# Front of a hybrid attention layer: value weights loaded and projected ahead of the queries and keys

## The chip, the cores and the metric

The kernel runs on one core of one Trainium2 chip. The metric is the device time of one execution in microseconds. Engines: PE is the tensor engine (matmuls and transposes), with its weight loads as PEld; DVE is the vector engine, ACT the scalar engine, POOL is GpSimd, and SP issues most DMAs. Each works through its own instructions in a fixed order; semaphores order the engines against each other.

## The reference

One layer over 1024 tokens of width 1024, all in float32:

```python
xn = rmsnorm(x, norm1_g[layer])
u = xn @ w_in[layer].astype(f32)
...
q_sb, k_sb, v_sb, f_raw, i_hg, q_hg, g_hg, gate_sb, gate_hg = jnp.split(u, list(c), axis=-1)
o_sb = stick_breaking_attention(split_heads(q_sb, SB_HEADS), split_heads(k_sb, SB_HEADS),
                                split_heads(v_sb, SB_HEADS))
...
merged = g_a * (o_sb @ w_o_sb[layer].astype(f32)) + g_b * (o_hg @ w_o_hg[layer].astype(f32))
h = x.astype(f32) + merged @ w_out[layer].astype(f32)
hn = rmsnorm(h, norm2_g[layer])
a = jnp.square(jax.nn.relu(hn @ w_ff1[layer].astype(f32)))
h = h + a @ w_ff2[layer].astype(f32)
```

A final `rmsnorm` follows. The change concerns the first two lines alone: the norm of the tokens, and the projections to the values of all 8 attention heads (512 columns of `w_in`) and to query and key of head 0 (64 columns each).

## The kernel before, in words

Tokens lie in 8 row blocks of 128 (`xt[0]` to `xt[7]`, tiles `x0` to `x7`), the width of 1024 in 8 k-blocks (`kt`). For full precision every operand of a projection is split into a high part in PE's format and a remainder: `hi_copy` casts on ACT (line 156), `lo_sub` subtracts on DVE (line 161), and a projection has three matmuls per k-block: high by high, remainder by high, high by remainder.

The front, for row blocks 0 to 3, goes like this. `first_norms` takes blocks 0 and 1: each block's sum of squares is made half on ACT (`n1scr`, line 629), half on DVE (line 281), added on DVE (`n_ms`, line 1284), raised to -1/2 on POOL (`n_y`, line 274), and multiplied into the block. `norm_transpose` has PE transpose the blocks into PSUM (`xnt`, one bank of PSUM for each k-block, line 131); ACT evicts the high part with the gain (`xnh`, line 348), DVE the remainder (`xnl`, line 351), both for two row blocks at once (256 columns). `u_qk0` is head 0's query and key weights (`wqk0r` as loaded, `wqk0whi` and `wqk0wlo` split), four DMAs of 128 KB; `u_v` the value weights, four tiles of 1024 columns (`wvr`, `wvh`, `wvl`, numbers 0 to 3), each with two k-blocks.

`first_job` writes PE's order of the projections as a generator; `st.advance(n, 1)` lets it go n steps on between the other stages. Before, it projects queries and keys (`pjqk`) of row blocks 0 and 1; then the values (`pjv`) of blocks 0 and 1 for the first four k-blocks, all matmuls with the high weights first, then those with the remainders; then queries and keys of blocks 2 and 3; then the other value k-blocks, and values of blocks 2 and 3. Row blocks 4 to 7 follow in the same way, half as many stages.

ACT and DVE stand in a fixed order in the front: `in_turn` chains each engine's instructions in the order in which they are written. `load` does the same for the DMAs of SP. An instruction that waits therefore holds up all that is written behind it on its engine. The order of the loads and of the stages is written out at the end of the kernel:

```python
    u_qk0.load()
    u_v.load(1)
    load_x(2)
    u_v.load(2)
    load_x(3)
    u_v.load()
...
    norm_transpose(xn, 0, 0, 2, lambda: keep_warm(1))
    st.advance(4, 1)
    u_v.split(2)
    norm1((2, 3), half_means((2, 3)))
```

Of the kernel before, what the change touches and what calls it, by code (L numbers as in the profile page):

```python
# [9 lines left out]
F32 = mybir.dt.float32  # L10
# [9 lines left out]
P = 128  # L20
# [19 lines left out]
def kernel(  # L40
# [230 lines left out]

    def inv_root(mean, name):
        y = small.tile([P, 1], F32, tag="rs_y1", name=f"{name}_y", bufs=4)
        nc.gpsimd.tensor_tensor(out=y, in0=mean, in1=expo[:, 0:1], op=ALU.pow)
        return y

    def mean_square(scr, src, before, name):
# [7 lines left out]
        )  # L285
        return out

    last_power = [None]

    last_evac = [None]  # L290

# [27 lines left out]
            c = (kt % 2) * 512 + (tb % 4) * P  # L319
            return h[:, c : c + P], l[:, c : c + P]  # L320

    def norm_transpose(acts, half, b0, n, between=None):

        banks = {}

        def turn_block(kt, b):
            if kt not in banks:
                banks[kt] = bank(f"xnt{half}{kt}_{b0}")[:, 0 : n * P]
            open_block("main")
            transpose(  # L330
                banks[kt][:, b * P : (b + 1) * P],
                xt[4 * half + b0 + b][:, kt * P : (kt + 1) * P],
            )

        ahead = 6 if between else 0
        for kt in range(ahead):
            turn_block(kt, 0)
        if between:
            between()
        for kt in range(KT):  # L340
            hi, lo = acts.t.get((half, kt // 2)) or acts.make(half, kt // 2)
            cs = slice(kt % 2 * 512 + b0 * P, kt % 2 * 512 + (b0 + n) * P)
            for b in range(n):
                if b > 0 or kt >= ahead:
                    turn_block(kt, b)
            pb = banks[kt]
            g = prm[:, G1 + kt : G1 + kt + 1]
            in_turn("act", nc.scalar.activation(hi[:, cs], pb, AF.Identity, scale=g))
            in_turn(
                "dve",  # L350
                nc.vector.scalar_tensor_tensor(
                    out=lo[:, cs],
                    in0=pb,
                    scalar=g,
                    in1=hi[:, cs].bitcast(F32),
                    op0=ALU.mult,
                    op1=ALU.subtract,
                ),
            )

    class Quads:

# [82 lines left out]
    class Unit:  # L445
# [192 lines left out]
    def first_norms(tbs):  # L638
        (l, lc), (r, rc) = halves()
        means = half_means(tbs)  # L640
        for tb in tbs:
            first = tb == tbs[0]
            if first:
                t = xt[tb][:, rc]
                in_turn("act", nc.scalar.activation(t, t, AF.Copy, scale=means[tb]))
# [12 lines left out]
    def norm1(tbs, means=None):  # L658
        for tb in tbs:
            t = xt[tb]  # L660
            r = means[tb] if means else token_rstd(t, f"n1_{tb}", slot(f"n1scr{tb}"))
            in_turn(
                "dve",
                nc.vector.tensor_scalar(out=t, in0=t, scalar1=r, scalar2=None, op0=ALU.mult),
            )
# [35 lines left out]
    class FirstUnit(Unit):  # L701
# [13 lines left out]
                ]  # L715

        def split(self, part=None):
            if part is None:
                return
            cs = slice(part * 512, (part + 1) * 512)  # L720
            (h, l), r = self.hl[0], self.raw[0]
            hi_lo(h[:, cs], l[:, cs], r[:, cs])

    def first_job():
        name, u_qk, ep = qk_item(0)
# [2 lines left out]
        u_v.roomy = range(4)  # L728
        open_banks = {}

        def v_part(tb, kt, hi=True, lo=True):
            if kt == 0 and hi:
                open_banks[tb] = bank(f"pjv_{tb}")
            ps = open_banks[tb]
            sh, sl = xn.stat(kt, tb)
            wh, wl = (w[:, kt % 2 * 512 : (kt % 2 + 1) * 512] for w in u_v.hl[kt // 2])
            if hi:
                matmul(ps, sh, wh, start=kt == 0, stop=False)
                matmul(ps, sl, wh, start=False, stop=False)
# [35 lines left out]
        return st.add([u_qk], body), u_qk, u_v  # L775

    j_first, u_qk0, u_v = first_job()
    j_qk = {0: j_first}

    QB_ORDER = (7, 0, 6, 1, 5, 2, 4, 3)  # L780
# [1546 lines left out]
    load_vectors(1, 6)  # L2327
    turns["on"] = True
    first_norms((0, 1))
    open_block("main")  # L2330
    keep_warm(1)
    norm_transpose(xn, 0, 0, 2, lambda: keep_warm(1))
    st.advance(4, 1)
    u_v.split(2)
    norm1((2, 3), half_means((2, 3)))
    lo_now()
    st.advance(3, 1)
    norm_transpose(xn, 0, 2, 2)
    u_v.split()
    st.advance(5, 1)  # L2340
    norm1(range(4, NT))
    st.advance(8, 1)
    norm_transpose(xn, 1, 0, 4)
# [169 lines left out]
```

## Time and profile before

| | us |
|---|---|
| three runs: median (lowest to highest) | 1420.89 (1420.53 to 1420.9) |
| the profiled execution: its own time | 1421.05 |
| the profiled execution: span | 1419.3 |
| PE busy | 1409.0 (99%) |
| DVE busy | 1087.3 (77%) |
| ACT busy | 684.4 (48%) |
| POOL busy | 147.9 (10%) |

Times in the profile's rows are microseconds from the start of the span. A row of the order of time has start, length, engine, source line, operation, output and inputs by the program's names without buffer numbers, shapes, and how many instructions it merges; a merged row's length reaches from the first start to the last end. In brackets stand the idle time of the engine just before, and what ended it. Matmuls overlap: one that lasts 0.39 us can be followed by the next after 0.23. So a busy PE is not PE at its peak, and paces are read from starts.

### The profile page before, as it was taken

The numbers are of one execution on the slowest core, as the hardware profiler recorded it, in microseconds if no ns is written. First come the engines' busy times: TensorE is split into PE (matmuls) and PEld (weight loads), VectorE is DVE, ScalarE is ACT, GpSimd is POOL, SyncE is SP. The second block draws the span as 40 slices with busy tenths as digits, with TensorE's granted clock in tenths as the row PEclk, the third lists the DMA queues.
The fourth block names the chain that finished last, engine by engine and source line by source line (L and its number), as shares of the span: only waits on it lengthen the run. The fifth ranks groups of instructions, "written<-read, shape, count | busy, mean of one in ns | idle before, by whom it ended". The sixth has DMA issues, their size and how long they took to land.

```text
span 1419.3 us, 18799 instructions
## 1 busy us (share of the span) xinstructions
PE 1409.0 (99%) x6848; PEld 1183.7 (83%) x6848; DVE 1087.3 (77%) x1494; ACT 684.4 (48%) x1181; POOL 147.9 (10%) x341
## 2 busy tenths in 40 slices
PE   9999999999999999999999999999999999999997
PEld 8888888888888888888888888888888888888886
DVE  7579988988567888887788897676666657768765
ACT  6356676664243554433344764445444443433343
POOL 3012223210011031000000300000000000000042
PEclk9999999999999999999999999999999999999999
DMA  7024445535135685364585514444446974776825
GB/s 243 26 67 127 106 99 98 107 77 155 60 74 174 221 223 182 123 213 156 163 297 193 185 58 166 163 163 145 140 141 242 355 259 154 275 278 239 275 98 179
DMA packets 163173, 237.72 MB, mean 167 GB/s; under 512 B 26332, under 2 KB 93448, under 8 KB 163080
## 3 DMA queue, kind: packets, MB, share of 16 engines
q1 hardware_dynamic: 146056, 190.37, 40.0%
q0 software_dynamic: 11584, 34.61, 10.0%
q10 hardware_dynamic: 5440, 11.54, 2.3%
q8 instruction: 54, 0.88, 0.2%
q14 instruction: 39, 0.32, 0.1%
HBM read 168.32 MB, written 66.06 MB: 165 GB/s over the span
## 4 chain that ended last, share of the span: by engine, by line
PE 98%; DVE 1%; ACT 1%; POOL 0%; DMA 0%; issue 0%; SPq 0%; DVEq 0%; ACTq 0%
PE pm L128 21%; PE pX L128 9%; PE pW L128 6%; PE pY L128 6%; PE pjqk L128 6%; PE pga L128 4%; PE gX L128 4%; PE gY L128 4%; PE pjf L128 3%; PE pjq L128 3%; PE pys L128 3%; PE pji L128 3%; PE pyh L128 3%; PE pjv L128 3%; PE po L128 3%; PE z L128 2%
## 5 line engine op out<-in xcount | busy, mean ns | idle before, releaser
L156 ACT CAST whid<-w 128x1024 fp32r<-128x1024 f32 x30 | 31.6, 1053 | 154.5 <-PE pm L128 89.8
L826 DVE TENSOR_TENSOR_SCAN rm<-rm,bits 128x511 f32<-128x511 f32 (+7 forms) x72 | 87.3, 1219 | 17.2 <-ACT rm L804 17.1
L128 PE MATMUL pm<-wlod,sh 128*128 128x512 f32 x240 | 93.5, 390 | 0.0
L128 PE MATMUL pm<-whid,sl 128*128 128x512 f32 x240 | 93.4, 389 | 0.0
L128 PE MATMUL pm<-whid,sh 128*128 128x512 f32 x240 | 93.4, 389 | 0.0
L128 PE MATMUL pm<-tl,sh 128*128 128x512 f32 (+1 forms) x210 | 81.3, 387 | 0.0
L128 PE MATMUL pm<-th,sl 128*128 128x512 f32 (+1 forms) x210 | 81.3, 387 | 0.0
L128 PE MATMUL pm<-th,sh 128*128 128x512 f32 (+1 forms) x210 | 81.3, 387 | 0.0
L161 DVE TENSOR_TENSOR wlod<-w,whid 128x1024 fp32r<-128x1024 f32 x30 | 36.7, 1222 | 55.2 <-ACT whid L156 55.1
L161 DVE TENSOR_TENSOR sl<-sa,sh 128x1024 fp32r<-128x1024 f32 x56 | 68.2, 1218 | 0.0
L156 ACT CAST wTh<-pw 128x512 fp32r<-128x512 f32 (+2 forms) x96 | 43.8, 485 | 41.9 <-PE pw L131 41.0
L2141 POOL TENSOR_SCALAR fss<-fss 128x1 f32<-128x1 f32 x8 | 4.5, 561 | 562.0 <-ACT fsc L2136 561.5
L156 ACT CAST sh<-sa 128x1024 fp32r<-128x1024 f32 x56 | 57.2, 1046 | 7.0 <-DMA sa<-ad 7.0
L128 PEld LDWEIGHTS pm<-wlod,sh 128*128 128x128 f32 x240 | 45.0, 187 | 9.9 <-DVE wlod L161 0.4
L128 PEld LDWEIGHTS pm<-whid,sh 128*128 128x128 f32 x240 | 45.1, 188 | 9.4
L161 DVE TENSOR_TENSOR wTl<-pw,wTh 128x512 fp32r<-128x512 f32 (+2 forms) x96 | 49.9, 546 | 3.9 <-ACT wTh L156 3.7
L128 PEld LDWEIGHTS pm<-whid,sl 128*128 128x128 f32 x240 | 45.1, 188 | 9.3
L169 DVE TENSOR_TENSOR bt<-bt,rm 128x511 f32<-128x511 f32 (+7 forms) x72 | 48.9, 684 | 3.5
L804 ACT ACTIVATE rm<-z 128x511 f32<-128x511 f32 (+4 forms) x96 | 48.0, 500 | 5.5 <-PE z L128 2.9
L128 PE MATMUL pX<-sql,t1h 128*128 128x512 f32 x128 | 49.9, 390 | 0.0
L128 PE MATMUL pX<-sqh,t1l 128*128 128x512 f32 x128 | 49.9, 390 | 0.0
L128 PE MATMUL pX<-sqh,t1h 128*128 128x512 f32 x128 | 49.8, 389 | 0.0
(930 smaller groups left out, 4435.9 us busy)
## 6 DMA issues: line engine op xcount, KB each, us to landing
w<-in_w_ff_dram SPq DMA_DIRECT2D x72, 512.0 KB, 4.8
sa<-ad SPq DMA_DIRECT2D x52, 512.0 KB, 6.4
ad<-a SPq DMA_DIRECT2D x32, 256.0 KB, 4.6
ad<-s SPq DMA_DIRECT2D x16, 512.0 KB, 3.3
tw<-in_w_out_dram POOLq DMA_DIRECT2D x24, 256.0 KB, 4.6
pr<-pd SPq DMA_DIRECT2D x10, 512.0 KB, 6.5
x<-in_x_dram SPq DMA_DIRECT2D x8, 512.0 KB, 7.8
xnl<-xnh POOLq DMA_DIRECT2D x8, 512.0 KB, 6.4
```

The costliest lines, as they stand in the source:

```text
L128: return pe(nc.tensor.matmul(*a, **k))
L156: hi_last[0] = after(in_turn("act", nc.scalar.copy(dst, src)), hi_behind[0])
L161: nc.vector.tensor_tensor(out=dst, in0=src, in1=hi.bitcast(F32), op=ALU.subtract),
L169: return nc.vector.tensor_tensor(out=out, in0=a, in1=b, op=ALU.mult)
L804: nc.scalar.activation(rm[:, s0 + c0 - 1 : s0 + m - 1], z[:, c0:m], AF.Sigmoid, scale=-0.125)
L826: sc = nc.vector.tensor_tensor_scan(out=rr, data0=rr, data1=bits[:, 1024 - nk + a : 1024 - nk + b][:, ::-1], initial=rm[:, b : b + 1] if i ...
L2141: nc.gpsimd.tensor_scalar(out=ssq, in0=ssq, scalar1=1.0 / D, scalar2=EPS, op0=ALU.mult, op1=ALU.add)
```

## The change

It reorders the front. (1) SP loads value weights 0 and 1 ahead of the query and key weights, and row blocks 2 and 3 behind those. (2) `first_norms` casts value weights 0 instead of the query and key weights; their remainders (`value_remainders`) are made half on DVE, half on POOL. (3) `norm_transpose` transposes all eight k-blocks of row block 0 before block 1, with two k-blocks in one PSUM bank (`paired`); value weights 1 are split between the fourth and the fifth k-block. (4) PE projects values of blocks 0 and 1 first, high weights, remainders of the tokens and remainders of the weights a quarter at a time (`v_quarter`), then queries and keys of blocks 0 and 1, then those of blocks 2 and 3 between the transposes of blocks 2 and 3. (5) The query and key weights are cast after the evictions; their remainders come on DVE after the mean of block 2. (6) The remainder of value weights 2 moves from DVE to POOL, and ACT takes half of block 3's norm.

```diff
@@ norm_transpose
+                pb = bank(f"xnt{half}{kt}_{b0}")
+                for i in range(1 + paired):
+                    banks[kt + i] = pb[:, i * n * P : (i + 1) * n * P]
...
-        ahead = 6 if between else 0
...
+            if then:
+                then(kt)
@@ Unit.split
-                if self.name == "wf1" or self.name == "wv" and i == 1:
+                if self.name == "wf1" or self.name == "wv" and i == 3:
                     hi_copy(h, r)
                     owed_wlo.append(lambda h=h, l=l, r=r: lo_sub(l, r, h))
                     continue
+                if self.name == "wv" and i == 2:
+                    hi_copy(h, r)
+                    ins = nc.gpsimd.tensor_tensor(
+                        out=l, in0=r, in1=h.bitcast(F32), op=ALU.subtract
+                    )
+                    after(ins, last_root[0])
+                    continue
@@ first_norms and what follows it
-        for part in range(2):
-            u_qk0.split(part)
+                split_values(0)
+
+    def split_values(i):
+        h, l = slot(f"wvh{i}", F32R), slot(f"wvl{i}", F32R)
+        u_v.hl = (u_v.hl or []) + [(h, l)]
+        raw = u_v.raw[i]
+        for _, cs in halves():
+            hi_copy(h[:, cs], raw[:, cs])
+
+    def value_remainders(i):
+        (h, l), raw = u_v.hl[i], u_v.raw[i]
+        (_, lc), (_, rc) = halves()
+        lo_sub(l[:, lc], raw[:, lc], h[:, lc])
+        nc.gpsimd.tensor_tensor(
+            out=l[:, rc], in0=raw[:, rc], in1=h[:, rc].bitcast(F32), op=ALU.subtract
+        )
@@ first_job
+        def v_quarter(k0):
+            for part in range(3):
+                for kt in (k0, k0 + 1):
+                    for tb in range(2):
+                        v_part(tb, kt, *(part == i for i in range(3)))
+                if part > 0:
+                    yield
...
         def body():
+            for k0 in (0, 2):
+                yield from v_quarter(k0)
             ps = bank(f"{name}_0")
             yield from qk_steps(ps, 0, 0, 2)
-            for hi in (True, False):
-                for k0 in (0, 2):
-                    for tb in range(2):
-                        for kt in (k0, k0 + 1):
-                            v_part(tb, kt, hi, not hi)
-                    yield
             yield from qk_steps(ps, 0, 2, 2)
@@ end of the kernel
+    u_v.load(2)
     u_qk0.load()
-    u_v.load(1)
     load_x(2)
-    u_v.load(2)
     load_x(3)
...
+    norm_transpose(xn, 0, 0, 2, lambda: keep_warm(1), second_values, 8, True)
+    for part in range(2):
+        u_qk0.split_hi(part)
+    means = half_means((2,))
+    for part in range(2):
+        u_qk0.split_lo(part)
+    means.update(half_means((3,)))
+    st.advance(8, 1)
+    u_v.split(3)
+    second_norms(means)
+    norm_transpose(
+        xn, 0, 2, 2, then=lambda kt: st.advance(1, 1) if kt in (4, 6, 7) else None, ahead=4
+    )
```

Where the instructions stand. First ACT, the evictions of row blocks 0 and 1, before; the two digits in `xnt00` are the half and the k-block, and the brackets name the engines whose semaphores an instruction waits for:

```order
L156 CAST wqk0whi_161<-wqk0r0_156 128x512 [waits DMAHW6_49,DMAHW5_49]
L348 ACTIVATE xnh00_229<-xnt00_0_216,prm_93 128x256 [waits PE_49]
L348 ACTIVATE xnh00_229<-xnt01_0_218,prm_93 128x256 [waits PE_49]
L348 ACTIVATE xnh01_237<-xnt02_0_220,prm_93 128x256 [waits PE_49]
L348 ACTIVATE xnh01_237<-xnt03_0_222,prm_93 128x256 [waits PE_49]
L348 ACTIVATE xnh02_245<-xnt04_0_224,prm_93 128x256 [waits PE_49]
```

The same place on ACT in the change:

```order
L156 CAST wvh0_210<-wvr0_156 128x512
L350 ACTIVATE xnh00_233<-xnt00_0_220,prm_93 128x256 [waits DVE_49,PE_49]
L350 ACTIVATE xnh00_233<-xnt00_0_220,prm_93 128x256 [waits DVE_49]
L350 ACTIVATE xnh01_241<-xnt02_0_223,prm_93 128x256 [waits PE_49]
L350 ACTIVATE xnh01_241<-xnt02_0_223,prm_93 128x256 [waits DVE_49]
L156 CAST wvh1_249<-wvr1_158 128x512 [waits DMAHW4_49]
L156 CAST wvh1_249<-wvr1_158 128x512
L350 ACTIVATE xnh02_255<-xnt04_0_226,prm_93 128x256 [waits PE_49]
```

Two evictions in a row now read one tile, and the second waits for DVE instead of PE; two casts stand among them.

On DVE, the mean of row block 2 in the change (`n1_2_ms` is DVE's half of it, `n1_2_ss` ACT's):

```order
L281 ISA n1scr2_273,n1_2_ms_276<-x2_167 128x512 [waits DMAHW1_49]
L281 ISA n1_2_ms_276 128x1
L1338 TENSOR_TENSOR n1_2_ms_276<-n1_2_ms_276,n1_2_ss_274 128x1 [waits DVE_49,Activation_49]
L161 TENSOR_TENSOR wqk0wlo_166<-wqk0r0_160,wqk0whi_165 128x512 [waits DMAHW6_49,DMAHW5_49]
L161 TENSOR_TENSOR wqk0wlo_166<-wqk0r0_160,wqk0whi_165 128x512 [waits DMAHW7_49,DMAHW0_49]
```

Before, the two `wqk0wlo` stood ahead of the first `xnl`, and values' remainders (`wvl0`) ahead of that mean; now `wqk0wlo` stands behind the sum that waits for ACT.

On PE, the first projection before:

```order
L131 MATMUL xnt07_0_260<-ident_75,x1_152 128x128
L128 MATMUL pjqk0_0_265<-xnh00_229,wqk0whi_161 128x256 [waits DVE_49]
L128 MATMUL pjqk0_0_265<-xnl00_230,wqk0whi_161 128x256
L128 MATMUL pjqk0_0_265<-xnh00_229,wqk0wlo_162 128x256
L128 MATMUL pjqk0_0_265<-xnh00_229,wqk0whi_161 128x256 [waits Activation_49]
```

and the end of the 24 value matmuls that stand in that place in the change, with the query and key matmuls behind them:

```order
L128 MATMUL pjv_0_217<-wvl1_250,xnh01_241 128x512 [waits Pool_49]
L128 MATMUL pjv_1_218<-wvl1_250,xnh01_241 128x512
L128 MATMUL pjqk0_0_315<-xnh00_233,wqk0whi_165 128x256 [waits Activation_49]
L128 MATMUL pjqk0_0_315<-xnl00_234,wqk0whi_165 128x256
L128 MATMUL pjqk0_0_315<-xnh00_233,wqk0wlo_166 128x256 [waits DVE_49]
L128 MATMUL pjqk0_0_315<-xnh00_233,wqk0whi_165 128x256
```

The first of these waits for ACT (the cast), the third for DVE (the remainder), each by itself.

More of the change, by code (lines that the diff above doesn't have):

```diff
@@ L273, in inv_root @@
         y = small.tile([P, 1], F32, tag="rs_y1", name=f"{name}_y", bufs=4)
-        nc.gpsimd.tensor_tensor(out=y, in0=mean, in1=expo[:, 0:1], op=ALU.pow)
+        last_root[0] = nc.gpsimd.tensor_tensor(out=y, in0=mean, in1=expo[:, 0:1], op=ALU.pow)
         return y
@@ L320, in stat, with norm_transpose @@
             return h[:, c : c + P], l[:, c : c + P]
-    def norm_transpose(acts, half, b0, n, between=None):
+    def norm_transpose(acts, half, b0, n, between=None, then=None, ahead=0, paired=False):
         banks = {}
@@ L327, in turn_block @@
             if kt not in banks:
-                banks[kt] = bank(f"xnt{half}{kt}_{b0}")[:, 0 : n * P]
+                pb = bank(f"xnt{half}{kt}_{b0}")
+                for i in range(1 + paired):
+                    banks[kt + i] = pb[:, i * n * P : (i + 1) * n * P]
             open_block("main")
@@ L342, in norm_transpose @@
             cs = slice(kt % 2 * 512 + b0 * P, kt % 2 * 512 + (b0 + n) * P)
-            for b in range(n):
-                if b > 0 or kt >= ahead:
-                    turn_block(kt, b)
+            for k in (kt, kt + 1)[: 1 + (kt + 1) % 2] if paired else (kt,):
+                for b in range(n):
+                    if (b > 0 or k >= ahead) and not (paired and kt % 2):
+                        turn_block(k, b)
             pb = banks[kt]
@@ L654, in first_norms, with second_norms, norm1 @@
                 turn_vectors(0, 1)
-        for part in range(2):
-            u_qk0.split(part)
-    def norm1(tbs, means=None):
+                split_values(0)
[12 more added lines that the diff above has]
+        )
+    def second_norms(means):
+        (l, lc), (r, rc) = halves()
+        for tb, cs in ((2, slice(None)), (3, lc)):
+            t = xt[tb][:, cs]
+            in_turn(
+                "dve",
+                nc.vector.tensor_scalar(
+                    out=t, in0=t, scalar1=means[tb], scalar2=None, op0=ALU.mult
+                ),
+            )
+        t = xt[3][:, rc]
+        in_turn("act", nc.scalar.activation(t, t, AF.Copy, scale=means[3]))
+    def norm1(tbs):
         for tb in tbs:
             t = xt[tb]
-            r = means[tb] if means else token_rstd(t, f"n1_{tb}", slot(f"n1scr{tb}"))
+            r = token_rstd(t, f"n1_{tb}", slot(f"n1scr{tb}"))
             in_turn(
@@ L729, in first_job, with open_bank, v_part @@
         open_banks = {}
-        def v_part(tb, kt, hi=True, lo=True):
-            if kt == 0 and hi:
-                open_banks[tb] = bank(f"pjv_{tb}")
+        def open_bank(tb):
+            open_banks[tb] = bank(f"pjv_{tb}")
+        def v_part(tb, kt, hi=True, mid=True, lo=True):
+            if kt == 0 and hi and tb not in open_banks:
+                open_bank(tb)
             ps = open_banks[tb]
```

38 lines of the change are left out of this document (23 added, 15 removed).

## The prediction

> **What bounds the kernel now.** I read the page first, then the busy time by stretches, then the order of time of the first 24 us. The page gives the span and the chain that ended last:
>
> ```profile
> span 1419.3 us, 18799 instructions
> ...
> PE 98%; DVE 1%; ACT 1%; POOL 0%; DMA 0%; issue 0%; SPq 0%; DVEq 0%; ACTq 0%
> ```
>
> The chain is the tensor engine (PE) nearly throughout, so a change counts only where it moves PE's idle time. The busy time by stretches says where PE has any (columns: length, then busy us and count for PE, PEld, DVE, ACT, POOL, then granted clock, DMA share, GB/s):
>
> ```profile
> 0.00:24.00 24.00, 21.27 (x130) 19.32 (x131) 18.04 (x40) 16.58 (x35) 5.26 (x15) 1.00 0.98 315
> 24.00:60.00 36.00, 35.96 (x174) 29.67 (x174) 23.40 (x54) 19.14 (x37) 7.20 (x15) 1.00 0.22 54
> 60.00:400.00 340.00, 339.65 (x1882) 291.99 (x1881) 278.34 (x406) 197.18 (x434) 58.96 (x195) 1.00 0.42 95
> ```
>
> After 24 us nothing is left to win, and nothing there can take up a delay either: what the front gains or loses reaches the end whole. The front in order of time (start, length, engine, what; in brackets the idle time before it and its releaser):
>
> ```profile
> 4.40 0.63 ACT L629 ACTIVATE n1scr<-x 128x512 f32<-128x512 f32 x1 [2.39 <-DMA x<-in_x_dram]
> ...
> 5.21 0.16 DVE L1284 TENSOR_TENSOR n_ms<-n_ms,n_ss 128x1 f32<-128x1 f32 x1
> ...
> 6.44 0.71 ACT L645 ACTIVATE x<-x,n_y 128x512 f32<-128x512 f32 x1
> ...
> 7.39 0.81 PEld L131 LDWEIGHTS xnt<-ident,x 128*128 128x128 f32 x6
> ...
> 8.16 0.30 PEld L128 LDWEIGHTS warm<-ident 128*128 128x128 f32 x2
> ...
> 8.42 1.09 PEld L131 LDWEIGHTS xnt<-ident,x 128*128 128x128 f32 x10
> 8.49 1.26 PE L131 MATMUL xnt<-ident,x 128*128 128x128 f32 x10
> 8.81 3.03 ACT L348 ACTIVATE xnh<-xnt,prm 128x256 fp32r<-128x256 f32 x8
> 9.49 3.22 DVE L351 SCALAR_TENSOR_TENSOR xnl<-xnt,prm,xnh 128x256 fp32r<-128x256 f32 x8
> ...
> 10.02 0.38 PE L128 MATMUL pjqk<-xnh,wqk0whi 128*128 128x256 f32 x1 [0.27 <-DVE xnl L351]
> ...
> 13.11 0.40 PE L128 MATMUL pjv<-wvh,xnh 128*128 128x512 f32 x1
> ...
> 16.77 1.07 PE L128 MATMUL pjv<-wvl,xnh 128*128 128x512 f32 x4
> ...
> 17.45 1.24 PEld L131 LDWEIGHTS xnt<-ident,x 128*128 128x128 f32 x10
> ...
> 18.10 3.03 ACT L348 ACTIVATE xnh<-xnt,prm 128x256 fp32r<-128x256 f32 x8 [3.15 <-PE xnt L131]
> 18.61 3.23 DVE L351 SCALAR_TENSOR_TENSOR xnl<-xnt,prm,xnh 128x256 fp32r<-128x256 f32 x8
> ...
> 20.97 0.28 PE L128 MATMUL pjqk<-xnh,wqk0whi 128*128 128x256 f32 x1
> ...
> 23.83 0.40 PE L128 MATMUL pjv<-wvh,xnh 128*128 128x512 f32 x1
> ```
>
> My yardstick is PE's time from its first projection (10.02) to the first matmul with value weights 2 (23.83): the change reorders what lies between and keeps all of it. Paces: a value matmul (16.77 - 13.11) / 16 = 0.229 us; a query/key matmul of 256 columns (23.83 - 20.97) / 24 = 0.119; a transpose 1.24 / 10 = 0.124. The work is 48 x 0.119 + 24 x 0.229 + 16 x 0.124 = 13.19 us out of 13.81, so PE idles 0.62 us there. That, and an earlier start, is all that can be won.
>
> **The change part by part.** *Loads.* The two value loads of 512 KB go ahead of the four small query/key loads. Two waits of ACT show when block 1 and the query/key weights land now; the queue's own rows show 512 KB landing every 1.3 to 1.4 us, since each issue waits for a landing eight transfers back:
>
> ```profile
> 5.81 0.63 ACT L629 ACTIVATE n1scr<-x 128x512 f32<-128x512 f32 x1 [0.69 <-DMA x<-in_x_dram]
> ...
> 8.19 0.62 ACT L156 CAST wqk0whi<-wqk0r 128x512 fp32r<-128x512 f32 x1 [0.46 <-DMA wqk0r<-in_w_in_dram]
> ...
> 13.51 0.33 SPq L136 DMA_DIRECT2D prow<-in_b_gate_dram  x1
> ...
> 14.86 1.60 SPq L136 DMA_DIRECT2D prow<-in_lb_logits_dram  x2
> ```
>
> Block 1 is in by 5.8, the query/key weights took 2.4 more. So value weights 0 and 1 land near 7.1 and 8.4, the query/key weights by 10.8, block 2 near 12.1, block 3 and the rest as before. ACT first wants these at 7.15 (6.44 + 0.71), 12.0, 15.9 and 16.9: covered, value weights 0 only just; they may be 0.9 us late, since ACT then idles from 8.3 (two casts) to 9.23. Cost nothing.
>
> *Start.* Eight instead of six transposes of block 0 run before block 1's: loads from 7.39 at 0.81 / 6 = 0.134 end at 8.46, the warm pair takes 0.26 (8.16 to 8.42), so block 1's matmuls start near 8.79 instead of 8.49. Both transposes of the first pair must be done: 8.91 + 0.32 (8.49 to 8.81) puts ACT's first eviction at 9.23, 0.42 later. But a value matmul with the high part wants that alone, where the query/key one waited for DVE: 9.23 + 0.49 + 0.05 = 9.77, 0.25 earlier.
>
> *Shared banks.* Two k-blocks now lie in one PSUM bank. In the order, every second eviction on ACT has got a wait for DVE that it didn't have. The rows nearest to it are the value evictions, two halves of one bank each:
>
> ```profile
> 34.22 0.37 ACT L156 CAST V<-pjv 128x256 fp32r<-128x256 f32 x1 [0.55 <-DVE V L161]
> ...
> 34.62 0.42 DVE L161 TENSOR_TENSOR V<-pjv,V 128x256 fp32r<-128x256 f32 x1 [0.44 <-ACT V L156]
> ...
> 35.34 0.43 DVE L161 TENSOR_TENSOR V<-pjv,V 128x256 fp32r<-128x256 f32 x1 [0.30 <-ACT V L156]
> 35.80 0.37 ACT L156 CAST V<-pjv 128x256 fp32r<-128x256 f32 x1 [0.49 <-DVE V L161]
> ```
>
> ACT starts 0.03 after DVE's end: strict turns. The Trainium skill, "PSUM — Partial Sum Buffer", section on PSUM bank collisions, says that no two engines may touch one bank at once, readers included, and that the chip does not arbitrate, so the program must. By that rule the turns are kept and the sum below stands; were columns enough to keep them apart, the sum would be rival one. The trace's turns agree with the rule.
>
> Durations of single instructions, in the groups by shape of the first 40 us (busy us, mean ns):
>
> ```profile
> L351 DVE SCALAR_TENSOR_TENSOR xnl<-xnt,prm,xnh 128x256 fp32r<-128x256 f32 x16 | 6.5, 476 | 0.0
> L348 ACT ACTIVATE xnh<-xnt,prm 128x256 fp32r<-128x256 f32 x16 | 6.1, 490 | 3.2 <-PE xnt L131 3.2
> ...
> L161 DVE TENSOR_TENSOR wqk0wlo<-wqk0r,wqk0whi 128x512 fp32r<-128x512 f32 x2 | 1.3, 684 | 0.0
> ...
> L156 ACT CAST wqk0whi<-wqk0r 128x512 fp32r<-128x512 f32 x2 | 1.2, 620 | 0.5 <-DMA wqk0r<-in_w_in_dram 0.5
> ```
>
> Back to back, evictions start (3.03 - 0.49) / 7 = 0.363 us apart; in turns, ACT to DVE is 0.51 (18.10 to 18.61) and DVE to ACT 0.476 + 0.03 = 0.51. Casts of 512 columns I take as 0.53 apart, between 0.49 (an overlap of 0.13, like the evictions') and 0.62. ACT's path: evictions at 9.23, 10.25, 10.61, 11.66; casts of value weights 1 at 12.02 and 12.55; evictions at 13.08, 14.10, 14.46, 15.51; casts of the query/key weights at 15.87 and 16.40; the square of block 2 at 16.93. The four turns cost 4 x (1.02 - 0.363) = 2.6 us, and the casts stand in the same queue.
>
> *The new wait.* On DVE the sum of block 2's mean waits for that square: 0.81 after its start (4.40 to 5.21), at 17.74. Queued behind it are the two subtractions that make wqk0wlo; the first starts at 17.84 and ends at 18.52. PE waits for it with its third query/key matmul.
>
> *PE's side.* Value matmuls: two at 9.77, then a wait for the second eviction until 10.25 + 0.54 = 10.79 (idle 0.56), then 22 x 0.229 to 15.83; value weights 1 are cast by 13.2, in time. The first query/key matmul waits for its cast until 15.87 + 0.67 = 16.54 (idle 0.71), two run, and the third waits until 18.57 (idle 1.79). Then 22 x 0.119 to 21.19. Blocks 2 and 3 are normalised by then (DVE at it from 19.9 to 21.5), eight transposes run, the first eviction can start at 22.0, and PE waits 0.11 for it and 0.38 for DVE's part (23.04). 23 x 0.119 + 6 x 0.124 end at 26.52.
>
> The sum: start -0.25, idle 3.55 instead of 0.62, +2.93: **+2.7 us** (26.52 against 23.83).
>
> *POOL* takes over half of two subtractions and all of the third (1024 columns). Nearest rows, both of two operands on POOL:
>
> ```profile
> L2151 POOL TENSOR_TENSOR y<-hb,gf 128x256 f32<-128x256 f32 x2 | 1.9, 960 | 1.0 <-DVE hb L1284 1.0
> ...
> L274 POOL TENSOR_TENSOR n_y<-n_ms,expo 128x1 f32<-128x1 f32 x4 | 3.0, 769 | 10.9 <-DVE n_ms L1284 10.9
> ```
>
> 512 columns: between 0.96 and 1.92. From 13.2 that is done by 15.1; PE wants it at 15.37. 1024 columns: between 0.96 and 3.84; from 20.9 done by 24.7, wanted at 26.98. I take the upper ends; both are hidden, the last by 2.3 us.
>
> *Behind.* ACT's evictions of blocks 2 and 3 end at 21.13 now (18.10 + 3.03), near 25.4 in the change, so the squares of blocks 4 to 7 come at most 4.3 us later. These rows show the slack:
>
> ```profile
> 29.34 0.75 DVE L664 TENSOR_SCALAR x<-x,n_y 128x1024 f32<-128x1024 f32 x1 [0.72 <-ACT wqk1h L156]
> ...
> 34.74 3.65 PE L131 MATMUL xnt<-ident,x 128*128 128x128 f32 x32
> ```
>
> The last normalised block is ready at 30.1 now, at 34.4 then, and is wanted at 37.4 (34.74 + 2.7). Hidden. Value weights 3 are cast from 25.4 and subtracted on DVE: twice the rows of 512 columns, 1.24 and 1.37, end at 28.0; PE wants them at 26.52 + 8 x 0.229 = 28.35. Thin cover: if DVE is 1 us later, PE loses 0.7.
>
> **The rivals.** One: *no turns in a bank, not slower.* If the new waits on ACT ask only for what DVE has done long before, the evictions go at 0.363: the query/key casts come at 13.2 and 13.7, wqk0wlo is ready by 15.9, and all behind it comes 2.7 us earlier: no change, 1420.9. It decides from the first pair on. For it: the order names the wait, not its count. Against it: the value evictions above. Better than -0.9 us it can't end: only 0.62 of idle time and 0.25 of start are there to win. Chance 0.10.
>
> Two: *PE falls back to its slow pace.* Near 16 to 18.6 PE stands 2.5 us with two matmuls between. PE starts slowly after standing still, as the first matmuls show (ns min/median/max):
>
> ```profile
> L128 PEld LDWEIGHTS warm<-ident x24: 190/333/333, 2.2 to 8.3; 128*128 128x128 f32 x24
> ```
>
> and their row in the order of time:
>
> ```profile
> 2.25 4.34 PEld L128 LDWEIGHTS warm<-ident 128*128 128x128 f32 x20 [2.25 <-POOL ident masks.py:199]
> ```
>
> They went 0.217 apart, later 0.11 (the pair at 8.16 lasts 0.30 with loads of 0.19). Half pace for another 4.3 us loses 2.2: +4.9 us, 1425.8. Against it: the longest stand now is under 0.5 us, so nothing shows that 2 us suffice. The Trainium skill, "TensorE: Matmul & The Clock Gate", Part 1, lets the clock halve only after an idle window of about 3.4 us; by that rule this stall is too short and the sum stands; no run here shows it. Chance 0.10.
>
> Three: *POOL is the late one*: above 6.1 us for 1024 columns the third subtraction ends after PE wants it; at twice my upper end, 7.7, that is 1.6 more, +4.3, 1425.2. Chance 0.04. That the change doesn't do what it says is ruled out by the order.
>
> **How the numbers follow.** The profiled execution took 1421.05 us with a span of 1419.3; the median of the three runs is 1420.89, 0.16 below it. The sum was made on the former and goes on the median: 1420.89 + 2.7 = 1423.6 us, chance 0.76. Its own range is +2.2 to +3.5: a dozen handovers at the shortest seen, a cast pitch of 0.49 to 0.62, the thin cover of value weights 3. 0.2% is 2.84 us, about what a measurement of this kernel can tell from no change, and lies in the middle of that range: half of it, 0.38, is over the bound. Slower: 0.38 + 0.10 + 0.04 = 0.52. Same: 0.38 and 0.08 of rival one, 0.46. Faster: 0.02, the rest of rival one, for what I don't see; no term reaches it. The range, 1422.3 to 1425.5, leaves out rival one and half of the other two.
>
> **What would show it.** Right: every second xnh of the first eight starts 0.5 us after an xnl, with ACT idle on DVE; PE's largest idle, near 1.8 us, ahead of a pjqk on wqk0wlo, with DVE's mean sum just before; the first pjv with value weights 2 near 26.5; from there on every time 2.7 later. Wrong: evictions 0.36 apart; pjqk 0.24 apart behind the stall (rival two); an idle PE released by POOL (rival three); or a difference that grows or shrinks after 30 us.

## The result and the profile after

The changed kernel takes 1425.85 us (median of 6 executions, 1425.15 to 1427.18); the kernel before, beside it, 1420.95 (median of 6, 1420.53 to 1421.09). The ratio is 1.0035 with a 95% interval of 1.0026 to 1.0045: 4.9 us slower, where the prediction said 2.7 and at most 4.6. The profiled execution took 1425.49 us, 4.44 more than that of before.

The page of the changed kernel, span and chain, and the busy time by the same stretches as in the kernel before (length, then busy us and count for PE, PEld, DVE, ACT, POOL, then granted clock, DMA share, GB/s):

```profile
span 1423.7 us, 18808 instructions
...
PE 97%; DVE 1%; ACT 1%; DMA 0%; POOL 0%; issue 0%; SPq 0%; ACTq 0%; POOLq 0%
```

```profile
0.00:24.00 24.00, 17.48 (x97) 14.88 (x98) 14.32 (x30) 12.88 (x27) 10.33 (x18) 1.00 0.97 311
24.00:60.00 36.00, 35.85 (x189) 30.19 (x187) 26.02 (x59) 20.05 (x40) 7.16 (x15) 1.00 0.18 42
60.00:400.00 340.00, 339.56 (x1876) 291.61 (x1876) 277.16 (x403) 200.28 (x437) 58.90 (x195) 1.00 0.42 97
```

PE is busy 17.48 us of the first 24 where it was busy 21.27: 3.8 us are lost there, 0.1 in the next 36 us, nothing behind. POOL is busy 10.33 us there instead of 5.26. What PE waited for in the first 60 us (total, times, longest; a wait of 2.2 us at the very start, the same in both kernels, is left out):

```profile
PE xnt L131 <- DVE x L689: 1.8, 1, 1.8
PE pjqk L128 <- DVE wqk0wlo L161: 1.4, 1, 1.4
PE pjv L128 <- ACT xnh L350: 0.5, 2, 0.3
PE pjqk L128 <- ACT wqk0whi L156: 0.5, 1, 0.5
```

The last three were forecast. The largest, on DVE's normalised x, was not. In the order of time:

```profile
6.47 0.48 DVE L660 TENSOR_SCALAR x<-x,n_y 128x512 f32<-128x512 f32 x1
...
8.10 1.14 ACT L156 CAST wvh<-wvr 128x512 fp32r<-128x512 f32 x2 [1.17 <-DMA wvr<-in_w_in_dram]
...
8.39 1.04 PE L131 MATMUL xnt<-ident,x 128*128 128x128 f32 x8
...
9.15 0.47 ACT L350 ACTIVATE xnh<-xnt,prm 128x256 fp32r<-128x256 f32 x1
...
9.67 0.73 PE L128 MATMUL pjv<-wvh,xnh 128*128 128x512 f32 x2 [0.24 <-ACT xnh L350]
...
10.17 0.84 ACT L350 ACTIVATE xnh<-xnt,prm 128x256 fp32r<-128x256 f32 x2 [0.55 <-DVE xnl L353]
...
13.16 1.30 POOL L679 TENSOR_TENSOR wvl<-wvr,wvh 128x512 fp32r<-128x512 f32 x1 [2.56 <-ACT wvh L156]
13.49 0.48 DVE L353 SCALAR_TENSOR_TENSOR xnl<-xnt,prm,xnh 128x256 fp32r<-128x256 f32 x1 [0.20 <-ACT xnh L350]
...
17.59 0.16 DVE L1338 TENSOR_TENSOR n_ms<-n_ms,n_ss 128x1 f32<-128x1 f32 x1 [0.56 <-ACT n1scr L640]
17.67 1.29 DVE L161 TENSOR_TENSOR wqk0wlo<-wqk0r,wqk0whi 128x512 fp32r<-128x512 f32 x2
...
18.41 0.39 PE L128 MATMUL pjqk<-xnh,wqk0wlo 128*128 128x256 f32 x1 [1.44 <-DVE wqk0wlo L161]
...
20.88 2.35 POOL L495 TENSOR_TENSOR wvl<-wvr,wvh 128x1024 fp32r<-128x1024 f32 x1
...
20.94 0.72 ACT L694 ACTIVATE x<-x,n_y 128x512 f32<-128x512 f32 x1 [1.84 <-POOL n_y L274]
20.94 2.57 DVE L689 TENSOR_SCALAR x<-x,n_y 128x512 f32<-128x512 f32 x1 [0.45 <-POOL n_y L274]
...
21.15 0.60 PE L131 MATMUL xnt<-ident,x 128*128 128x128 f32 x4
...
23.57 0.87 PE L131 MATMUL xnt<-ident,x 128*128 128x128 f32 x6 [1.82 <-DVE x L689]
23.93 1.94 ACT L350 ACTIVATE xnh<-xnt,prm 128x256 fp32r<-128x256 f32 x5 [2.27 <-PE xnt L131]
...
28.64 0.40 PE L128 MATMUL pjv<-wvh,xnh 128*128 128x512 f32 x1
```

The row to stop at is DVE's at 20.94. It multiplies half of block 3 by its root, 128x512, and takes 2.57 us. The same operation on half of block 0, at 6.47, takes 0.48. It waits for nothing: its idle time before, 0.45, is ended by the root. It is simply long, from 0.06 us after POOL begins its subtraction of value weights 2 (20.88) to 0.28 after POOL ends it (23.23 and 23.51). ACT's half of the same block, at the same time, takes its 0.72. If something holds DVE here, the trace shows it as a long instruction, not as a wait.

The first matmul with value weights 2 starts at 28.64 instead of 23.83, 4.81 later; the profiled execution is 4.44 longer. The difference is still 4.8 at about 1110 us (1111.7 against 1106.9 for the same matmul) and 4.4 at about 1400 us; where those 0.4 us go was not pursued.

### The profile page after: what moved, and what is told of

It is laid out like the page before. It is cut to its first block, busy times and chain, and to the rows that moved or that the text cites. A ratio compares the mean times of both kernels' runs of the same rounds, so it can differ in the third digit from the quotient of the medians.

```text
span 1423.7 us, 18808 instructions
## 1 busy us (share of the span) xinstructions
PE 1409.5 (99%) x6848; PEld 1183.7 (83%) x6848; DVE 1087.7 (76%) x1493; ACT 685.9 (48%) x1184; POOL 149.7 (11%) x344
## 4 chain that ended last, share of the span: by engine, by line
PE 97%; DVE 1%; ACT 1%; DMA 0%; POOL 0%; issue 0%; SPq 0%; ACTq 0%; POOLq 0%
PE pm L128 21%; PE pX L128 9%; PE pW L128 6%; PE pY L128 6%; PE pjqk L128 6%; PE pga L128 4%; PE gX L128 4%; PE gY L128 4%; PE pjf L128 3%; PE pjq L128 3%; PE pys L128 3%; PE pji L128 3%; PE pyh L128 3%; PE po L128 3%; PE pjv L128 3%; PE z L128 2%
```

## Experiments

The theory after this reading, H: POOL's subtraction holds DVE's norm of block 3, and this is the 2.1 us that the prediction missed. Rivals: the norm is slow for its own reasons (A), or PE's clock costs the time (B). Times are medians with lowest and highest; the kernel before, timed beside each group, had medians of 1421.07 to 1421.12 us, up to 0.17 above the 1420.95 of the first measurement. Differences from the changed kernel are between such groups.

**e1, e2, e3: the hold.** In e1 the two routes of the remainder become one:

```
-                if self.name == "wf1" or self.name == "wv" and i == 3:
+                if self.name == "wf1" or self.name == "wv" and i in (2, 3):
...
+    lo_now()
     u_v.split()
```

> The changed kernel, with the remainder of value weights 2 (1024 columns) taken from POOL and given to DVE behind its last eviction of blocks 2 and 3. Theory H (held): POOL's subtraction holds DVE's norm of block 3 for as long as it runs. Then the norm (128x512, 2.57 us in the changed kernel) falls to 0.48, as in the kernel before at the same shape, PE's wait of 1.8 us for x goes, and the time falls by 1.4 to 2.1 us against the changed kernel, to about 1424.0. Rival A (own cause): the norm is slow because ACT works on the other half of the same tile, or for its own operands; it stays above 2 us and the time stays within 0.5 us of the changed kernel. Rival B (clock): PE's slow spell, not the norm, costs the missing 2 us; the norm may fall, but the time falls by less than 0.7 us.

In e2 ACT takes both halves of block 3's norm:

```
-        for tb, cs in ((2, slice(None)), (3, lc)):
+        for tb in (2,):
...
-        t = xt[3][:, rc]
-        in_turn("act", nc.scalar.activation(t, t, AF.Copy, scale=means[3]))
+        for cs in (lc, rc):
+            t = xt[3][:, cs]
+            in_turn("act", nc.scalar.activation(t, t, AF.Copy, scale=means[3]))
```

> The changed kernel, with both halves of block 3's norm on ACT, one after the other; POOL's subtraction of 1024 columns stays. Theory H: what POOL's subtraction holds is DVE only. ACT's halves take 0.7 us each as the one in the changed kernel, block 3 is ready 1.0 to 1.2 us earlier (about 22.3 instead of 23.5), and the time falls by 0.8 to 1.3 us against the changed kernel. Rival C (memory): POOL's subtraction slows whoever uses the memory; ACT's halves are stretched above 1 us each and the gain is under 0.4 us.

In e3 POOL gets half:

```
-                        out=l, in0=r, in1=h.bitcast(F32), op=ALU.subtract
+                        out=l[:, lc], in0=r[:, lc], in1=h[:, lc].bitcast(F32), op=ALU.subtract
...
+                    owed_wlo.append(
+                        lambda h=h, l=l, r=r: lo_sub(l[:, rc], r[:, rc], h[:, rc])
+                    )
```

> The changed kernel, with only the first 512 columns of value weights 2's remainder on POOL (1.3 us by POOL's other subtractions), the other 512 on DVE behind its last eviction of blocks 2 and 3. Theory H: the norm of block 3 ends with POOL's subtraction, so it takes 1.3 to 1.6 us instead of 2.57, PE's wait for x falls from 1.8 to about 0.8, and the time falls by 0.8 to 1.2 us against the changed kernel. Rival D (fixed price): meeting POOL costs DVE's norm a fixed time; it stays near 2.5 us and the time within 0.5 us.

Rows of e1, e2 and e3 in the order of time:

```profile
21.09 0.48 DVE L689 TENSOR_SCALAR x<-x,n_y 128x512 f32<-128x512 f32 x1 [0.44 <-POOL n_y L274]
...
26.73 0.40 PE L128 MATMUL pjv<-wvh,xnh 128*128 128x512 f32 x1
...
27.53 0.50 PE L128 MATMUL pjv<-wvl,xnh 128*128 128x512 f32 x1 [0.16 <-DVE wvl L161]
```

```profile
21.00 2.37 POOL L495 TENSOR_TENSOR wvl<-wvr,wvh 128x1024 fp32r<-128x1024 f32 x1
21.06 1.34 ACT L695 ACTIVATE x<-x,n_y 128x512 f32<-128x512 f32 x2 [1.83 <-POOL n_y L274]
```

```profile
20.77 1.27 POOL L496 TENSOR_TENSOR wvl<-wvr,wvh 128x512 fp32r<-128x512 f32 x1
...
20.84 1.49 DVE L693 TENSOR_SCALAR x<-x,n_y 128x512 f32<-128x512 f32 x1 [0.44 <-POOL n_y L274]
```

Without POOL beside it the norm takes 0.48; with a POOL instruction half as long, 1.49; and on ACT, beside POOL's 2.37, each half takes its ordinary time. The length of the norm is POOL's length and a quarter of a microsecond. A is out, and so are a fixed price (D) and a contention for memory that slows every engine (C).

The times: e1 1425.58 (1423.90 to 1426.40), e2 1423.91 (1423.36 to 1425.52), e3 1424.98 (1424.62 to 1425.25). e2 and e3 are 1.9 and 0.9 below the changed kernel. That is more for e2 than the 0.8 to 1.3 forecast: ACT takes the half first that DVE had, so this half is ready near 21.8 instead of 23.5, and PE does not wait for x at all. The median of e1 fell by 0.3 only, which is what B said, not the 1.4 to 2.1 of H. Its lowest is 1.25 below the lowest of the changed kernel, its profiled execution 1.12 below the profiled one, and at the first matmul with value weights 2 it is 1.91 earlier (26.73 against 28.64), of which PE loses part again behind the remainder that DVE now makes late (27.53). So H holds for the norm, but the executions of e1 lie 2.5 us apart, and something else is in them.

**e4: the same meeting in the kernel before.** Only the remainder of value weights 1 goes to POOL, behind the root of block 3:

```
+                            lambda h=h, l=l, r=r: after(
+                                nc.gpsimd.tensor_tensor(
+                                    out=l, in0=r, in1=h.bitcast(F32), op=ALU.subtract
+                                ),
+                                last_root[0],
+                            )
```

> The kernel before, with one edit: the remainder of value weights 1 (1024 columns, 1.22 us on DVE) runs on POOL behind the root of block 3's mean, so that it meets DVE's norm of block 3 (128x1024, 0.75 us before). Theory H: that norm takes about as long as POOL's subtraction, 2.3 to 2.6 us, and blocks 2 and 3 are transposed later; the time rises by 0.5 to 2 us. Rival A: the norm stays at 0.75 us; POOL's subtraction, about 2.4 us, ends at 19.2 instead of 18.7 and the time stays within 0.6 us.

```profile
16.39 2.52 POOL L490 TENSOR_TENSOR wvl<-wvr,wvh 128x1024 fp32r<-128x1024 f32 x1
16.76 2.70 DVE L674 TENSOR_SCALAR x<-x,n_y 128x1024 f32<-128x1024 f32 x1
```

The norm of 128x1024, 0.75 us in the kernel before, takes 2.70; PE waits 1.6 us for it, and the one execution took 1422.38, 1.3 more than the kernel before. The hold belongs to the meeting, not to the new order. The norm ends 0.55 us after POOL here (18.91 and 19.46), and 0.28 after it with half the columns in the changed kernel, so it had done little before POOL ended.

**e5 to e8: the other terms.** e5 is e1 with DVE's order changed:

```
-    means = half_means((2,))
     for part in range(2):
         u_qk0.split_lo(part)
-    means.update(half_means((3,)))
+    means = half_means((2, 3))
```

> The changed kernel with value weights 2's remainder on DVE (as in e1) and, besides, the two subtractions that make wqk0wlo put ahead of block 2's mean on DVE. Theory S (several late things): the wait of PE's third query/key matmul falls from 1.4 to 0.1 us, but DVE's means of blocks 2 and 3 end as late as before, since DVE does the same work in another order; PE then waits for x of block 2 and 3 instead, and the time falls by only 0.2 to 0.6 us against e1. Rival E (the mean's wait is the cause): the order on DVE alone costs the 1.3 us, and the time falls by 1.0 to 1.4 us against e1.

e6 gives each k-block its bank (and puts six transposes ahead instead of eight):

```
-    norm_transpose(xn, 0, 0, 2, lambda: keep_warm(1), second_values, 8, True)
+    norm_transpose(xn, 0, 0, 2, lambda: keep_warm(1), second_values, 6)
```

> The changed kernel with one PSUM bank for each k-block of row blocks 0 and 1 (six transposes ahead instead of eight), all else kept, POOL's subtraction of value weights 2 too. Theory T (turns): the first eight evictions go 0.36 us apart and everything behind them on ACT comes 2.4 to 2.7 us earlier, so the waits for the query/key cast (0.5 us) and for wqk0wlo (1.4 us) go; DVE's norm of block 3 is still held by POOL's subtraction, now some 2.5 us earlier, and PE waits 1 to 2 us for it. The time falls by 1.8 to 2.6 us against the changed kernel, to 1423.3 to 1424.0. Rival F (not the turns): the evictions are late through the casts of value weights among them or through transposes; the time falls by less than 0.8 us.

e7 is the edits of e6 and e1 together, e8 those of e6, e5 and e1.

> e6 with value weights 2's remainder on DVE as in e1: no turns and nothing of POOL beside the norm. Theory T with theory H: both stalls of PE go, and what the order saves at the start is left: 1420.3 to 1421.6 us, within 0.6 us of the kernel before or better than it, and the runs lie within 0.6 us of each other. Rival G (order): projecting values first costs time by itself, say through block 2 and 3 becoming late; the time stays 1.5 us or more above the kernel before.

> e7 with wqk0wlo ahead of block 2's mean on DVE too. Theory T with theory H: with the turns gone, wqk0wlo is in time either way, so this is within 0.3 us of e7. Rival E: the wait of the mean costs PE time in e7 as well, and this is 0.5 us or more faster than e7.

e5 took 1423.93 (1423.58 to 1424.25). In its profile PE's wait for wqk0wlo is 0.2 instead of 1.4 us, and a new one, 0.5 us for x of block 2, stands behind it; the profiled execution is 0.44 below that of e1, the lowest one 0.32. That is theory S (several things are late at once); the median, 1.65 below the scattered one of e1, is not used for it. e6 took 1423.03 (1422.55 to 1424.61), 2.8 below the changed kernel. Its rows:

```profile
8.92 1.55 ACT L350 ACTIVATE xnh<-xnt,prm 128x256 fp32r<-128x256 f32 x4
...
18.00 2.59 DVE L689 TENSOR_SCALAR x<-x,n_y 128x512 f32<-128x512 f32 x1 [0.44 <-POOL n_y L274]
...
20.64 0.88 PE L131 MATMUL xnt<-ident,x 128*128 128x128 f32 x6 [1.49 <-DVE x L689]
```

Four evictions in 1.55 us, 0.36 apart, and both waits for the query/key weights are gone; the norm is held as before, 2.9 us earlier. e7, without either, took 1421.73 (1421.55 to 1422.04; ratio 1.0005, 0.9996 to 1.0013), 0.1 above the forecast of T (the turns) with H, and e8 1421.93 (1421.69 to 1422.33): the mean's place on DVE no longer matters once the turns are gone, as T said and E (the mean's wait) did not. Taken in this order, the turns are worth 2.8 us and the hold 1.3. What is left of the new order, values ahead of queries, is 0.6 us above the kernel before in e7, by its interval anything from -0.6 to 1.8.

**e9, e10: what a stand of PE costs.** Executions of the kernels in which PE stands 1.4 us or more at a time lie far apart (e1 2.5 us, e2 2.2, e6 2.1, the changed kernel 2.0); those of e5, e7 and e8, with stands of 0.5 at most, lie within 0.7. e3 is an exception: stands of 1.4 and 0.7, and executions within 0.6. The profiles of all these kernels show full clock in this stretch, so the spread alone does not name its cause. The clock was tested by itself, in e7 with a longer stand: the query/key casts come last on ACT, the first half several times over.

```
+    means = half_means((2, 3))
+    u_v.split(3)
+    second_norms(means)
-    for part in range(2):
+    for part in (0, 0, 0, 0, 0, 0, 0, 1):
         u_qk0.split_hi(part)
```

> The kernel of e7 (no stall of PE above 0.5 us) with the query/key weights cast last on ACT, behind block 3's norm, and their first half cast seven times over with the same result, so that PE stands still for 5 to 6 us ahead of its first query/key matmul. Theory K (clock): after a stand that long PE's clock is granted at half speed for some time, and query/key matmuls then go 0.24 apart instead of 0.12; the time rises by the stand and 1.4 to 2.2 us more, and the runs with stands of 1.4 to 1.8 us (the changed kernel, e1, e2, e6) scatter because some of them fall into this. Rival L (no clock): the matmuls go 0.12 apart from the first on, no granted clock below 1.00 in this stretch, and the time rises by the stand alone.

> e9 with the first half cast twice instead of seven times: PE stands still for 2.5 to 3.2 us. Theory K: some executions fall to half clock and others don't, so the runs lie in two groups 1.3 to 2 us apart, 3 us and some 4.7 us above e7. Rival L: the runs lie within 0.6 us of each other.

e9 took 1429.04 (1428.92 to 1429.72), 7.3 above e7. Its query/key matmuls in the order of time, and its busy time by stretches:

```profile
21.73 0.58 PE L128 MATMUL pjqk<-xnh,wqk0whi 128*128 128x256 f32 x1 [5.64 <-ACT wqk0whi L156]
...
22.83 0.42 PE L128 MATMUL pjqk<-xnh,wqk0whi 128*128 128x256 f32 x1
...
25.19 0.37 PE L128 MATMUL pjqk<-xnh,wqk0wlo 128*128 128x256 f32 x1
25.40 0.28 PE L128 MATMUL pjqk<-xnh,wqk0whi 128*128 128x256 f32 x1
...
26.34 0.28 PE L128 MATMUL pjqk<-xnh,wqk0wlo 128*128 128x256 f32 x1
```

```profile
18.50:21.70 3.20, 0.00 (x0) 0.00 (x0) 0.00 (x0) 3.07 (x6) 0.00 (x0) 0.51 1.08 350
21.70:25.30 3.60, 3.57 (x16) 3.48 (x17) 2.43 (x3) 0.50 (x1) 0.00 (x0) 0.50 0.75 140
25.30:28.00 2.70, 2.68 (x21) 2.25 (x20) 0.39 (x1) 0.90 (x3) 0.00 (x0) 0.98 0.51 111
```

The granted clock falls to 0.5 in the middle of the stand and stays there for 3.6 us of work. Eleven matmuls go 0.215 apart (22.83 to 25.19), the next eight 0.118. From 21.73 to 25.40 run 15 of them and a transpose, 15 x 0.119 + 0.124 = 1.91 us of work in 3.67: 1.76 lost. With the stand of 5.64 that makes 7.4, against 7.3 measured. K (the clock falls) holds for a long stand. e10, with a stand of 2.4 us and full clock in its profile, took 1425.03 with executions from 1423.64 to 1425.94 and no clean gap: three with a mean granted clock of 0.999 up to 1424.54, four with 0.997 or 0.998 from 1425.03 on. The spread rules out L (executions within 0.6) and agrees with K, but the groups lie 0.5 and 0.9 us lower than K said and are less sharp.

**e11: the subtraction twice.**

```
                     after(ins, last_root[0])
+                    after(
+                        nc.gpsimd.tensor_tensor(
+                            out=l, in0=r, in1=h.bitcast(F32), op=ALU.subtract
+                        ),
+                        ins,
+                    )
```

> The changed kernel with POOL's subtraction of value weights 2 made twice in a row, the second writing the same values again. Theory H1 (held for one instruction): DVE's norm of block 3 gets its turn when the first subtraction ends and takes 2.5 to 2.7 us as before; the second subtraction starts only when the norm is done or lasts longer. Theory H2 (held while POOL is at it): the norm ends with the second subtraction and takes about 4.9 us, and the time rises by 2.3 us against the changed kernel.

```profile
21.48 2.35 POOL L495 TENSOR_TENSOR wvl<-wvr,wvh 128x1024 fp32r<-128x1024 f32 x1
...
21.55 2.57 DVE L695 TENSOR_SCALAR x<-x,n_y 128x512 f32<-128x512 f32 x1 [0.44 <-POOL n_y L274]
...
23.91 2.42 POOL L500 TENSOR_TENSOR wvl<-wvr,wvh 128x1024 fp32r<-128x1024 f32 x1
```

H1: the norm is held for one POOL instruction, 2.57 us again, and runs when that one ends. This one execution took 1427.13, as long as the longest of the changed kernel, and its busy time by stretches shows the larger part of the reason:

```profile
20.80:24.20 3.40, 1.58 (x15) 1.35 (x13) 2.87 (x2) 0.72 (x1) 3.32 (x3) 1.00 1.05 244
24.20:27.60 3.40, 3.40 (x17) 3.23 (x17) 2.05 (x5) 2.05 (x6) 2.13 (x1) 0.54 0.70 157
```

Up to the norm this is the changed kernel. PE stands 1.82 us for x, is busy 1.58 of 3.40 us, and then works for about 3.4 us at half clock. The first matmul with value weights 2 comes at 30.28, 1.64 later than in the changed kernel; 0.61 of that stood already before the norm (21.55 against 20.94), so the half clock cost about 1.0. So a stall like the changed kernel's own can bring the clock down; its profiled execution, with the same stall, kept 1.00, as did that of e10 with its longer stand, so the length of one stand does not decide it. Among the six executions of the changed kernel, three lie at 1425.15 to 1425.54 with a mean granted clock of 0.999, and three at 1426.16 to 1427.18 with 0.998 or 0.997. That these three fell to half clock is likely, not shown: none of the profiles is of one of them, and a low mean alone does not price it, for the three executions of e3 with 0.997 are at most 0.6 us above its shortest.

**e12: what the runs suggest, in one kernel.** The edit of e6, DVE's order of e5, one `st.advance(1, 1)` behind the sixth k-block's evictions, so that eight value matmuls go ahead of the last transposes, and POOL's subtraction behind the norm:

```
     u_v.split(3)
-    second_norms(means)
+    last_norm = second_norms(means)
+    tc.add_manual_dep(lo_now().ins, last_norm.ins.name, SYNC, reason="behind the norm")
```

> What the runs suggest, in one kernel: the changed order with a bank for each k-block (e6), wqk0wlo ahead of block 2's mean (e5), the last two k-blocks' transposes put behind the first eight value matmuls (in e7 they made PE wait 0.4 us for a bank), and value weights 2's remainder on POOL again, but behind DVE's norm of block 3 instead of beside it. Theory T with theory H: the norm takes 0.48 us and POOL's subtraction, beside evictions only, costs nothing; the first value matmul comes near 9.6 instead of 10.1, and the time is 0.3 to 0.9 us below e7, at 1420.8 to 1421.4, the same as the kernel before. Rival M: POOL's subtraction holds DVE's evictions too; they take over 1 us each and the time is above e7.

```profile
9.60 1.19 PE L129 MATMUL pjv<-wvh,xnh 128*128 128x512 f32 x4 [0.27 <-ACT xnh L353]
...
16.91 1.31 DVE L693 TENSOR_SCALAR x<-x,n_y 128x1024 f32<-128x1024 f32 x2 [0.17 <-POOL n_y L277]
...
18.36 2.37 POOL L499 TENSOR_TENSOR wvl<-wvr,wvh 128x1024 fp32r<-128x1024 f32 x1 [0.66 <-issue]
...
19.78 3.04 DVE L356 SCALAR_TENSOR_TENSOR xnl<-xnt,prm,xnh 128x256 fp32r<-128x256 f32 x7 [1.56 <-ACT xnh L353]
```

1421.00 us (1420.60 to 1421.57), ratio 1.0000 (0.9991 to 1.0009): the time of the kernel before, with the new order. Both norms together take 1.31. Seven of DVE's evictions take 3.04, the same as in e7, where POOL is idle then; the first two or three of them lie beside POOL's subtraction, which ends at 20.73. The kernel can have the subtraction on POOL without a wait, behind the norm from 18.36 on instead of beside it. It does not beat the kernel before. Its executions lie 1.0 us apart with no stand above 0.3, so half of a spread of 2 us can come without any stand.

## Why the prediction was wrong

*Loads* held only by luck. Value weights 0 came 0.95 us later than forecast (ACT's cast at 8.10 instead of 7.15, idle 1.17), which the text had as 0.9 and covered by the transposes. But these began at 8.39 instead of 8.79, and ACT goes from the late cast to the first eviction with no idle time between. In e5, where the eviction does wait for PE, it comes 0.42 after that start, so 8.8 would have done here: by this estimate the load cost 0.3 us, and the earlier transposes paid for it. In e11 ACT's cast began at 8.71 and the first value matmul came at 10.28 instead of 9.67.

*Start* and *Shared banks* held to 0.1 us, the start with that luck. First eviction 9.15 (forecast 9.23), first value matmul 9.67 (9.77), then ACT in turns with DVE: the second eviction at 10.17 (10.25), the third behind it in the same row. e6 puts the price of the turns at 2.8 us of the median, 2.6 of the lowest; the term said 2.6 on ACT's path.

*The new wait* held: mean sum 17.59 (17.74), wqk0wlo 17.67 (17.84), third query/key matmul 18.41 (18.57). e5 adds what the sum didn't say: with that wait gone, PE stands for block 2 instead, and only some 0.4 us come back. The wait was late ACT work in another place.

*PE's side* held until block 2's transposes, 21.15 (21.19), and failed one row later. "Blocks 2 and 3 are normalised by then (DVE at it from 19.9 to 21.5)": DVE was at it until 23.51. **This is the step that failed.** An end at 21.5 gives the norm of block 3 its ordinary time, 0.48 us for 128x512, which is what it takes with POOL's subtraction out of the way (e1), while the change puts POOL's longest instruction of this stretch right beside it. The first eviction came at 23.93 instead of 22.0, and the end of the yardstick at 28.64 instead of 26.52: of the miss of 2.12 us, 1.93 stand at that eviction and come from this one row. With the subtraction on DVE instead (e1) the yardstick ends at 26.73, and the three shortest of its seven executions take 1423.9 to 1424.4 us, against the forecast 1423.6; the other four are longer, as said above.

*POOL* had the durations right and the question wrong. 1.28 and 1.30 us for 512 columns lie in 0.96 to 1.92, 2.35 for 1024 in 0.96 to 3.84, and the result was in time. "Both are hidden" asked only who waits for POOL's result, not whom POOL keeps from working. The Trainium skill, "SBUF — State Buffer", section on who interferes with whom, says it: DVE and POOL share a pair of ports; a `tensor_scalar` from SBUF to SBUF can take both pairs, whoever starts first keeps the shared one for the whole instruction, and the other blocks. The runs agree in every point that they touch: the norm is held to POOL's end (2.57, 1.49, 2.70), ACT is not (1.34 for two), an eviction that reads PSUM is not (0.48 at 13.49), and the hold is one instruction long (e11). e12 keeps the two apart, so it does not test a norm that starts first. That page should have been a rival with a price.

The kernel before had the sign of it, from the other side. A POOL instruction on 128x1 (line 265) takes 0.19 us as a rule there (median of 12). Beside DVE's norms of later row blocks:

```profile
25.18 0.75 DVE L664 TENSOR_SCALAR x<-x,n_y 128x1024 f32<-128x1024 f32 x1 [0.72 <-POOL n_y L269]
25.23 0.75 POOL L265 TENSOR_SCALAR n_ss<-n_ss 128x1 f32<-128x1 f32 x1
...
26.70 0.19 POOL L265 TENSOR_SCALAR n_ss<-n_ss 128x1 f32<-128x1 f32 x1
```

The norm starts first, keeps its 0.75, and POOL's short instruction takes 0.75 too, ending 0.05 after it; the pair at 27.87 and 27.92 does the same. At 26.70, 0.05 after another norm, POOL kept its 0.19. So a reader of these rows could have asked what a long POOL instruction that starts first does to a norm.

*Rival two* was nearer than its 0.10, but its figure, 1425.8, is the measured one by coincidence: the profiled execution, 1425.49, has full clock throughout this stretch, and what it lost beyond the forecast is the norm. The median lies 0.36 above that execution, most likely because in some executions PE works a stretch at half clock; that is the rest between 4.44 and 4.9 (the other 0.10 is the kernel before, whose median lies that much below its profiled execution). The chance was argued down with the rule of "TensorE: Matmul & The Clock Gate", Part 1 of the Trainium skill, that the clock halves after an idle window of about 3.4 us. Here the measurements differ: in e11 it halved after a stretch of 3.4 us in which PE had worked 1.58. The measurement decides. When exactly it halves, and why e3's executions lie close together all the same, stays open.

*Rival one* fell: e6 shows what the kernel would be without turns. *Rival three* (POOL late) did not occur. *Behind* held: no new wait of PE behind 30 us.

## What to carry to other kernels

When work moves to POOL, list what DVE does at that time and ask of each instruction whether POOL holds it; a row for a DVE instruction taken with POOL idle does not price the same instruction beside POOL. Put the POOL instruction behind the short DVE one. And a stand of PE can have a second price, half clock for a while behind it (about 1.0 us in e11, 1.76 in e9). After a stand of 1.8 us that seems to come in some executions only: look at the spread of the times, not at one profile.

## What the runs showed of the hardware

- A POOL subtraction in SBUF (2.35 us, 128x1024) held a DVE `tensor_scalar` in SBUF for its whole length: 0.48 became 2.57 us, 0.75 became 2.70, and with half the columns on POOL 1.49. DVE evictions from PSUM beside a POOL subtraction and ACT instructions beside it kept their times (0.48 and 0.72).
- The other way round, a POOL instruction on 128x1 of 0.19 us took 0.75 beside a DVE norm of 0.75 that had started 0.05 us earlier, in two of three meetings (kernel before).
- PE's granted clock was 0.54 over a stretch of 3.4 us behind a stand of only 1.82 us (e11), and 0.50 for 3.6 us of work behind one of 5.64 (e9), where it cost 1.76 us; behind a stand of 2.40 us it stayed at 1.00 (the profile of e10).
- Two engines that take turns in one bank took 1.02 us for each pair of 128x256 evictions on ACT's side (9.15 to 10.17), where separate banks took 0.36 (four in 1.55).
